# One transformer layer on one core: h, o and the merged tile in four tiles per half, o loaded block pair by block pair, and three merge weights split on VectorE

## The chip, the cores and the metric

The kernel runs on one core of a Trainium2 chip. A core has TensorE (matrix products into PSUM), VectorE, ScalarE and GpSimd (elementwise work), SyncE, whose queue issues most transfers, and 16 DMA engines shared by the transfer queues of SyncE, ScalarE and GpSimd. Each engine works through its own instructions in order and waits on semaphores for the others.

The metric is the device time of one execution in microseconds, the median of three. The profile is of one more execution. In its rows PE is TensorE, PEld its weight loads, DVE VectorE, ACT ScalarE, POOL GpSimd and SPq the transfers issued by SyncE; L12 is line 12 of the kernel.

## The reference

One layer works on 512 latent tokens (a grid of 8 x 64) and on 128 context tokens. Both groups go through the same weights. Cut to what matters here:

```python
h = _rmsnorm(x, p["norm1_g"]) * (1.0 + sc1) + sh1
u_rw, u_na, gate_rw, gate_na = jnp.split(h @ p["w_in"], IN_SPLITS, axis=-1)
o_rw, s_new = _rwkv_branch(u_rw, s0, ...)     # bidirectional recurrence, 8 heads of 64
q, k, v = jnp.split(u_na, 3, axis=-1)
...
o_na = _na_latent(q, k, v, ctx_k, ctx_v, p["na_rpb"])   # neighbourhood attention
merged = (jax.nn.sigmoid(gate_rw) * (o_rw @ p["w_o_rwkv"])
          + jax.nn.sigmoid(gate_na) * (o_na @ p["w_o_na"]))
x = x + g1 * (merged @ p["w_out"])
h2 = _rmsnorm(x, p["norm2_g"]) * (1.0 + sc2) + sh2
x = x + g2 * ((jax.nn.silu(h2 @ p["ffn_w1"]) * (h2 @ p["ffn_w3"])) @ p["ffn_w2"])
```

D_MODEL is 1024, so h, the merged tile and o (o_na and o_rw side by side, 512 features each) have 1024 features for 640 tokens.

## The kernel before

**High and low halves.** Every large product is made of three: an operand x is kept as hi, its rounding to TensorE's fast float format, and lo = x - hi, and w.x is hi.hi + hi.lo + lo.hi. So every activation tile comes twice. Features lie on the partitions: 1024 features are 8 blocks of 128, and a block has 640 columns, one for each token.

**h, o and m share their room.** The pool `hp` holds, one after the other, h (hi in `hh`, lo in `hl`), o (`o[0]`, `o[1]`) and the merged tile (`mh`, `ml`). Each of these is a `Two`: two tiles of four blocks (`hp_t`, line 334, `Two`, line 337, `hilo`, line 345). A tile of o takes the buffer of the tile of h with the same tag, and so can be loaded only when the last reader of that tile of h is done. o itself has waited in DRAM (`o_d`), since h is still needed while it is made; block 7 stays on the chip (`o3`).

**The stage around the change.** The recurrence goes through four channel groups ct, each in turn `main` (products for the chunk matrices), `inv` (inverting 32 x 32 blocks row by row on VectorE, 30 steps), `carry` (the sequential part) and `out` (normalisation, gate). TensorE's idle time between these is filled by a stream of independent products, `stream(order)`: projections (k, r, v, l), gates g0 to g15, then the merge products a0 to a3 (o_na by w_o_na, blocks 0 to 3 of o) and b0 to b3 (blocks 4 to 6). The table `plan` says how many products of the stream each step takes (`weave`), `tick` and `later` put the elementwise work of a product a few products behind it. The orders of TensorE, VectorE, ScalarE and GpSimd are those in which the program is written; a scheduler sets SyncE's.

**The last gate.** g14 is the last reader of h. Alone among the gates it goes through the blocks by pairs (`gate2_gen`, line 570): for each pair of blocks kts both halves of the tokens, six products each. After the pairs (0, 1) and (2, 3) it calls `o_load(0, 4)`, which issues eight transfers (hi and lo of blocks 0 to 3, 320 KB each). Blocks 4 and 5 are loaded when a0 is written (line 812), block 6 when the recurrence has stored it.

**Weights.** `wdma` (line 157) loads 512 KB into one of two buffers `wst`; `wcast` (line 178) makes hi by a ScalarE cast (line 185) and lo in one of two ways. With "p" in the table `wl`, ScalarE writes -w (line 183) and a GpSimd transfer of 512 KB adds w to it (line 184, `wlo<-wst` in the profile). With "d", VectorE subtracts (line 188). The buffer `wst` is free when cast and low half are done, and so the load of the weight after next waits for them. `wl` has one letter for each of the 39 units of the stream; letters 32 to 35 are those of a0 to a3.

In ct = 3 the lines to follow are: L579 the products of g14, L216 those of a and b, L1484 the loads of o, L164 the loads of merge weights, L1262 the transpose with which `inv` starts, L1293 and L1297 its steps, L1306 and L1308 the transposes at its end, L1137 and L1139 the bonus term, L1122, L1444, L1445, L1446 and L1448 the normalisation of the channel group before, L1216, L1239, L1188 and L1191 products for the chunk matrices (L1222 copies out the first of them), L1453 the gate product, L1319 and L1333 the products that join the inverted blocks, L1327 and L1338 the copies of the result.

Of the kernel before, what the change touches and what calls it, by code (L numbers as in the profile page):

```python
# [8 lines left out]
F32R = mybir.dt.float32r  # L9
# [5 lines left out]
P = 128  # L15
NT = 640
# [54 lines left out]
    h2=0.91, jobs=((2, 9, 28), (2, 9, 28), (2, 9, 28), (2, 8, 28)),  # L71
    mds=((4, 12), (4, 12), (4, 12), (4, 12)), bud=((1.8, 0.8), (1.3, 1.8)), off=6, tk=2, h3=1,
    h4=1.07, g1=2, km="dddddddd", kb="ddpd", ma="d", yo="pppd", r0="pd", rl=(0, 0, 0), lh=(0, 0, 1, 1),
    wl="dddddddddppppppppppppppppppppppppppdddd", nu=9, lg=14, jo=(2, 0, 1), na=(
        "6.0.12.0.1 6.0.12.0.0 6.0.12.0.0 6.0.12.0.2 6.0.12.0.0 6.0.12.0.2 6.0.12.0.0 6.0.12.0.2 6.0.12.0.0 "
        "6.0.12.0.2 6.0.12.1.0 6.1.12.1.2 6.2.12.2.0 6.1.12.2.2 6.0.12.2.0 6.1.12.1.2 6.2.14.2.0 "
        "6.2.14.1.2 6.2.14.2.0 6.2.14.2.0 6.3.18.2.0 10.0.10.0.0"))
# [30 lines left out]
def body(ctx: ExitStack, tc: tile.TileContext, xs, xp, cols, consts, w_ada, b_row, w_rw, w_qkv,  # L108
# [10 lines left out]
    def right_pool(stack, name):  # L119
        return stack.enter_context(tc.tile_pool(name=name, bufs=1, reuse_waits="tile", side="right"))  # L120
# [4 lines left out]
    hp = right_pool(hstack, "hp")  # L125
# [9 lines left out]
    def nm(s):  # L135
        cn[0] += 1
        return f"{s}_{cn[0]}"
# [34 lines left out]
    def later(fn, cost=(0.5, 0), more=0):  # L172
        if off[0]:
            pend.append([off[0] + more, cost, fn])
        else:
            fn()
# [155 lines left out]
    o, mt = [], []  # L332

    def hp_t(n, i, j):
        return hp.tile([P, 4, NT], F32R, tag=f"hp{i}{j}", bufs=1, name=f"{n}{i}{j}")

    class Two:

# [1 line left out]
            self.ts = ts  # L340

        def __getitem__(self, x):
            return self.ts[x[1] // 4][x[0], x[1] % 4, x[2]]

    def hilo(n):
        return [Two([hp_t(n, i, j) for j in range(2)]) for i in range(2)]

    hh, hl = hilo("h")

    s0 = ExitStack()  # L350
# [219 lines left out]
    def gate2_gen(i, w, ps_, gsb, gtag):  # L570
        dst = trw_d[i] if i < 8 else tna_d[i - 8]
        ps = [ps_(), None]
        for kts in ((0, 1), (2, 3), (4, 5), (6, 7)):
            for hf, (a, b) in enumerate(halves):
                if ps[hf] is None:
                    ps[hf] = ps_()
                for kt in kts:
                    for n, (u, x) in enumerate(((w[0], hh), (w[0], hl), (w[1], hh))):
                        pe.matmul(ps[hf][:, :H2], u[:, kt * 128:kt * 128 + 128], x[:, kt, a:b],  # L579
                                  start=kt == 0 and n == 0, stop=kt == 7 and n == 2)  # L580
                        yield
            if kts[1] == 3:
                o_load(0, 4)

        def rest(hf, a, b):
            t = gsb.tile([P, H2 if gtag == "fl" else 643], F32, tag=gtag, bufs=2, name=nm(gtag))[:, :H2]
            act.activation(t, ps[hf][:, :H2], AF.Tanh, scale=0.5)
            sp.dma_start(dst[:, a:b], t)

        for hf, (a, b) in enumerate(halves):  # L590
            later(lambda hf=hf, a=a, b=b: rest(hf, a, b))
# [192 lines left out]
    def stream(order):  # L784
# [10 lines left out]
        for i, g in enumerate(order):  # L795
            while wait.get(g) not in marks:
                yield False
            n, f = us[i][0], us[i][3]
            cast(i)
            it = f(ws[i])  # L800
            for j in range(n):
                if j == n // 8:
                    later(lambda i=i: cast(i + 1), (1.05, 0), -off[0])
                if j == (n // 2 if n == 48 else n // 4) and i + 2 < len(us):
                    ds.append(us[i + 2][1]())
                next(it)
                tick(1)
                if j == n - 1:
                    drain(it)
                    done.add(g)  # L810
                    if g == "a0":
                        o_load(4, 6)
                        if "O2" in marks:
                            o_load(6, 7)
                yield True
# [7 lines left out]
    with s1:  # L823
# [93 lines left out]
        with ExitStack() as s1b:  # L917
# [127 lines left out]
            with tc.manual_schedule(engines=FIRST):  # L1045
                for k, step in enumerate(PRM["na"].split()):
                    a, p, b, q, n = (int(x) for x in step.split("."))
# [29 lines left out]
    with ExitStack() as s3:  # L1077
# [397 lines left out]
        def o_load(a, b):  # L1475

            if not o:
                o.extend(Two([]) for _ in range(2))
            for q in sorted(set(range(a, b)) - got):
                got.add(q)  # L1480
                for i, (t, t_d) in enumerate(zip(o, o_d)):
                    if len(t.ts) == q // 4:
                        t.ts.append(hp_t("o", i, q // 4))
                    sp.dma_start(t[:, q, :].bitcast(F32), t_d[q])  # L1484

        def mt_tile(c8):
# [152 lines left out]
    pp = open_pool(ctx, "pp4", bufs=3, space=PSUM)  # L1639

    mh, ml = hilo("m")
    def last_gen():
        ts_ = []
# [44 lines left out]
    def add_gated(ps, i, n, c, a=0, b=512):  # L1688
# [15 lines left out]
                      name=f"b{x[0]}{x[1]}{i}") for i in range(2)] for x in halves2}  # L1704
# [390 lines left out]
```

## Time and profile before

| | us |
|---|---|
| median of 3 runs | 1171.59 (1171.57 to 1172.24) |
| the profiled execution, its own time | 1170.39 |
| its span, first to last instruction | 1168.6 |
| TensorE busy in the span | 1123.1 |
| VectorE busy | 775.6 |
| ScalarE busy | 535.4 |
| GpSimd busy | 194.3 |
| mean granted TensorE clock | 0.992 |

The profiled execution's own time is 1.2 us below the median of the three runs. A row of a timeline gives the start, the time, the engine, the line, the operation, what it writes and reads, and in brackets how long the engine had been idle before and what ended that; products are pipelined, so their times overlap. A row of a table by stretches gives for each engine the busy time and the number of instructions, then the clock granted to TensorE, the busy share of the DMA engines and the rate.

### The profile page before, as it was taken

To read this page: it belongs to the slowest core of one execution; us is meant where nothing else is said; L and a number is where in the kernel's file an instruction comes from. 1 tells how busy PE (TensorE), PEld (TensorE's weight loads), DVE (VectorE), ACT (ScalarE), POOL (GpSimd) and SP (SyncE) were. 2 spreads that over 40 slices of the span, in tenths; PEclk is the share of its full clock that TensorE was granted. 3 is DMA by queue.
4 is the path that set the end of the run, shared out by engine and by line. 5 is a ranking of instruction groups with operands and counts; after the bars stand their busy time and mean duration, and the time that the engine had idled before them with its cause. 6 is when DMAs were issued, how large, how long until landed. Compare 5 with 4: busy or idle time off the path is not lost.

```text
span 1168.6 us, 26884 instructions
## 1 busy us (share of the span) xinstructions
PE 1123.1 (96%) x11160; PEld 995.0 (85%) x11160; DVE 775.6 (66%) x1639; ACT 535.4 (46%) x1054; POOL 194.3 (17%) x264
## 2 busy tenths in 40 slices
PE   6999999999999999999899899989999999999998
PEld 4688877789888988888788778989899989998997
DVE  4565365569558847945577856877567756875775
ACT  4444566554565665557353424644224423441330
POOL 1163244320101212110200241100000000001000
PEclk9999999999999999999999999999999999999999
DMA  9752777654433433343843772322212321232122
GB/s 338 259 117 81 229 245 226 200 145 117 110 85 88 133 82 91 105 107 91 276 130 108 239 217 67 96 73 85 97 54 91 100 87 67 73 108 90 54 83 98
DMA packets 60770, 150.21 MB, mean 129 GB/s; under 512 B 7492, under 2 KB 22468, under 8 KB 60648
## 3 DMA queue, kind: packets, MB, share of 16 engines
q1 hardware_dynamic: 55464, 131.56, 34.4%
q0 software_dynamic: 4320, 15.73, 6.9%
q8 instruction: 88, 1.44, 0.5%
q10 hardware_dynamic: 864, 1.20, 0.4%
q14 instruction: 34, 0.28, 0.1%
HBM read 118.41 MB, written 14.32 MB: 114 GB/s over the span
## 4 chain that ended last, share of the span: by engine, by line
PE 60%; DVE 7%; issue 7%; ACT 3%; DMA 1%; SPq 0%; POOL 0%; DVEq 0%; ACTq 0%; POOLq 0%
PE f L1814 23%; PE acc L303 16%; PE fl L216 10%; DVE pr L1293 1%; PE mm L216 1%; PE w L1394 1%; DVE RL L1297 1%; PE w L1367 1%; PE w L1191 1%; PE w L1407 1%; DMA o<-o_d 1%; PE w L1379 1%; PE w L1169 1%; ACT wlo L183 1%; PE w L1239 0%
## 5 line engine op out<-in xcount | busy, mean ns | idle before, releaser
L1814 PE MATMUL f<-t,whi 128*128 128x320 f32 x640 | 141.4, 309 | 0.0
L1814 PE MATMUL f<-b,whi 128*128 128x320 f32 x608 | 136.4, 312 | 3.6 <-ACT b L204 1.8
L303 PE MATMUL acc<-whi,u 128*128 128x512 f32 (+1 forms) x448 | 135.9, 385 | 0.0
L216 PE MATMUL fl<-h,whi 128*128 128x320 f32 x672 | 121.3, 320 | 0.8 <-issue 0.8
L1814 PEld LDWEIGHTS f<-t,whi 128*128 128x128 f32 x640 | 106.9, 188 | 0.0
L1814 PEld LDWEIGHTS f<-b,whi 128*128 128x128 f32 x608 | 102.7, 189 | 4.7 <-ACT b L204 2.2
L216 PEld LDWEIGHTS fl<-h,whi 128*128 128x128 f32 x672 | 101.5, 188 | 5.5 <-issue 0.9
L185 ACT CAST whi<-wst 128x1024 fp32r<-128x1024 f32 (+1 forms) x77 | 79.1, 1033 | 56.1 <-PE acc L303 42.5
L1814 PE MATMUL f<-t,wlo 128*128 128x320 f32 x320 | 98.9, 309 | 0.0
L303 PEld LDWEIGHTS acc<-whi,u 128*128 128x128 f32 x448 | 83.5, 188 | 16.6
L1814 PE MATMUL f<-b,wlo 128*128 128x320 f32 x304 | 94.6, 311 | 1.4 <-DVE wlo L1858 1.4
L1855 ACT CAST whi<-ws 128x1024 fp32r<-128x1024 f32 x40 | 42.0, 1050 | 108.4 <-PE f L1814 48.2
L303 PE MATMUL acc<-wlo,u 128*128 128x512 f32 (+1 forms) x224 | 86.3, 385 | 0.0
L1869 POOL TENSOR_TENSOR ws<-wst 128x512 f32<-128x512 f32 x20 | 28.0, 1402 | 341.3 <-DVE wlo L1858 247.7
L188 DVE TENSOR_TENSOR wlo<-wst,whi 128x1024 fp32r<-128x1024 f32 (+2 forms) x55 | 58.3, 1072 | 31.8 <-ACT whi L185 31.2
L303 PE MATMUL acc<-whi,h 128*128 128x512 f32 x240 | 78.5, 401 | 0.8 <-DVE h L428 0.8
L1691 DVE SCALAR_TENSOR_TENSOR tt<-acc,G 128x512 f32<-128x512 f32 (+1 forms) x51 | 34.7, 680 | 59.3 <-PE acc L303 45.3
L216 PE MATMUL fl<-h,wlo 128*128 128x320 f32 x336 | 63.5, 321 | 0.0
L1855 ACT CAST whi<-wst 128x1024 fp32r<-128x1024 f32 (+1 forms) x48 | 41.3, 868 | 42.3 <-PE acc L303 25.1
L1814 PEld LDWEIGHTS f<-t,wlo 128*128 128x128 f32 x320 | 60.1, 188 | 0.0
L1858 DVE TENSOR_TENSOR wlo<-ws,whi 128x1024 fp32r<-128x1024 f32 x40 | 55.0, 1374 | 6.3 <-ACT whi L1855 6.3
L1814 PEld LDWEIGHTS f<-b,wlo 128*128 128x128 f32 x304 | 57.6, 190 | 1.7 <-DVE wlo L1858 1.7
(342 smaller groups left out, 2512.8 us busy)
## 6 DMA issues: line engine op xcount, KB each, us to landing
wst<-in_w_dram SPq DMA_DIRECT2D x66, 512.0 KB
wst<-in_w_rw_dram SPq DMA_DIRECT2D x31, 512.0 KB
wlo<-wst POOLq DMA_DIRECT2D x30, 512.0 KB, 4.6
wa<-in_w_ada_dram SPq DMA_DIRECT2D x24, 512.0 KB
f<-in_w_ada_dram SPq DMA_DIRECT2D x16, 512.0 KB
wst<-in_w_qkv_dram SPq DMA_DIRECT2D x12, 512.0 KB
o<-o_d SPq DMA_DIRECT2D x14, 320.0 KB
x<-in_xs_dram SPq DMA_DIRECT2D x8, 512.0 KB
```

What stands on the lines that cost most here:

```text
L183: act.activation(lo[:, :n], st[:, :n], AF.Copy, scale=-1.0)
L185: act.copy(hi[:, :n], st[:, :n])
L188: dve.tensor_tensor(out=lo[:, a:b], in0=st[:, a:b], in1=hi[:, a:b].bitcast(F32), op=ALU.subtract)
L216: pe.matmul(ps[:, :t1 - t0], w[:, a:a + 128], x[:, k0 + kt, t0:t1], start=n == 0, stop=n == 3 * nk - 1)
L303: pe.matmul(pss[i][:, a:b], lhs(x, kt, ts_), w[:, cs_], start=ki == 0 and n == 0, stop=ki == last and n == 2)
L1169: pe.matmul(t[r0:r0 + 32, 64 * i:64 * i + 64], S.BK[l // 10][own, l % 10, 0, 32 * bk:32 * bk + 32], V(AG[own, l, h, :], [[0, 2], [1, 32]], ...
L1191: pe.matmul(pr[h][hrows[h ^ i], o_], x[hrows[h], :], R_[hrows[h], l, :], start=True, stop=True)
L1691: dve.scalar_tensor_tensor(out=tt, in0=ps[:, a:b], scalar=c, in1=G[:, g, sl], op0=ALU.mult, op1=ALU.mult)
L1814: pe.matmul(ps[:, :H2], w_[:, c_], x_[:, kt, :], start=first and kt + n == 0, stop=last and kt == 3 and n == 2, skip_group_check=more)
L1855: act.copy(r[0][:, :width], src())
L1858: dve.tensor_tensor(out=r[1][:, :width], in0=src(), in1=r[0][:, :width].bitcast(F32), op=ALU.subtract)
L1869: eng_x(PRM["se"][i - 1]).tensor_tensor(out=o_, in0=x, in1=y, op=op)
```

## The change

Three edits. The tiles of the pool `hp` have two blocks instead of four, so h, o and m are four tiles each for hi and lo, in the same room. The loads of o are issued in pairs: after g14 has used blocks 0 and 1 the four transfers of these blocks, after blocks 2 and 3 theirs; the loads of blocks 4 and 5 keep their place in the program but now need only the third tile of h. And in `wl` the letters of a0, a1 and a2 become "d": their low halves are made by VectorE, without the ScalarE copy and the GpSimd transfer.

```diff
@@ PRM
-    wl="dddddddddppppppppppppppppppppppppppdddd", ...
+    wl="dddddddddppppppppppppppppppppppdddpdddd", ...
@@ hp_t, Two, hilo
-        return hp.tile([P, 4, NT], F32R, tag=f"hp{i}{j}", bufs=1, name=f"{n}{i}{j}")
+        return hp.tile([P, 2, NT], F32R, tag=f"hp{i}{j}", bufs=1, name=f"{n}{i}{j}")
...
-            return self.ts[x[1] // 4][x[0], x[1] % 4, x[2]]
+            return self.ts[x[1] // 2][x[0], x[1] % 2, x[2]]
...
-        return [Two([hp_t(n, i, j) for j in range(2)]) for i in range(2)]
+        return [Two([hp_t(n, i, j) for j in range(4)]) for i in range(2)]
@@ gate2_gen
-            if kts[1] == 3:
-                o_load(0, 4)
+            if kts[1] < 4:
+                o_load(kts[0], kts[0] + 2)
@@ o_load
-                    if len(t.ts) == q // 4:
-                        t.ts.append(hp_t("o", i, q // 4))
+                    while len(t.ts) <= q // 2:
+                        t.ts.append(hp_t("o", i, len(t.ts)))
```

TensorE's order is the same product by product. Two queues change. First SyncE's, at the loads of o, with what each transfer waits for (PE, DVE, Activation: the counters of those engines; DMAHW and DMASW with a number: an earlier transfer of SyncE's and of GpSimd's queue). Before:

```order
L1484 DMA o_7606<-o_d_81 128x640 [waits PE_49]
L1484 DMA o_7604<-o_d_80 128x640 [waits DMAHW7_49,PE_49]
L1484 DMA o_7604<-o_d_80 128x640 [waits DMAHW0_49]
L1484 DMA o_7606<-o_d_81 128x640 [waits DMAHW1_49]
L1484 DMA o_7604<-o_d_80 128x640 [waits DMAHW2_49]
L1484 DMA o_7606<-o_d_81 128x640 [waits DMAHW3_49]
L1484 DMA o_7604<-o_d_80 128x640 [waits DMAHW4_49]
L1484 DMA o_7606<-o_d_81 128x640 [waits DMAHW5_49]
L164 DMA wst_7926<-in_w_o_dram 128x2x512 [waits DMAHW6_49,DMASW6_49,Activation_49]
L588 DMA tna_d<-fl_7731 128x320 [waits DMAHW7_49,Activation_49]
```

And with the change:

```order
L1484 DMA o_7587<-o_d_81 128x640 [waits PE_49]
L1484 DMA o_7585<-o_d_80 128x640 [waits DMAHW7_49,PE_49]
L1484 DMA o_7585<-o_d_80 128x640 [waits DMAHW0_49]
L1484 DMA o_7587<-o_d_81 128x640 [waits DMAHW1_49]
L164 DMA wst_7930<-in_w_o_dram 128x2x512 [waits DMAHW2_49,DVE_49]
L1484 DMA o_7615<-o_d_81 128x640 [waits DMAHW3_49,PE_49]
L1484 DMA o_7613<-o_d_80 128x640 [waits DMAHW4_49,PE_49]
L1484 DMA o_7613<-o_d_80 128x640 [waits DMAHW5_49]
L1484 DMA o_7615<-o_d_81 128x640 [waits DMAHW6_49]
L1484 DMA o_7946<-o_d_81 128x640 [waits DMAHW7_49,PE_49]
L1484 DMA o_7943<-o_d_80 128x640 [waits DMAHW0_49,PE_49]
```

The load of a2's weight (`wst<-in_w_o_dram`) now stands between the two groups of four and waits for VectorE (a0's low half) where it waited for ScalarE and GpSimd's transfer; blocks 4 and 5 follow at once, ahead of g14's stores (`tna_d<-fl`).

Second VectorE's order, in `inv` of ct = 3 at the fifth and sixth steps. Before:

```order
L1293 TENSOR_TENSOR pr_7596<-RL_7560 128x65 x2
L1297 TENSOR_TENSOR RL_7560<-RL_7560,pr_7596 128x13x5 x2
L1139 TENSOR_TENSOR bv_7329<-w_7716,vp_623 128x320
L1293 TENSOR_TENSOR pr_7596<-RL_7560 128x72
L1293 TENSOR_TENSOR pr_7596<-RL_7560 128x78
```

And with the change:

```order
L1293 TENSOR_TENSOR pr_7605<-RL_7564 128x65 x2
L1297 TENSOR_TENSOR RL_7564<-RL_7564,pr_7605 128x13x5 x2
L188 TENSOR_TENSOR wlo_7744<-wst_7611,whi_7743 128x1024
L1139 TENSOR_TENSOR bv_7333<-w_7721,vp_627 128x320
L1293 TENSOR_TENSOR pr_7605<-RL_7564 128x72
```

The low half of a1 has come in ahead of the bonus term. Those of a0 and a2 stand, in the same way, right behind the transpose of L1262 and at step 17 of the inversion (128x119), each as one row more.

More of the change, by code (lines that the diff above doesn't have):

```diff
@@ L73 @@
     h4=1.07, g1=2, km="dddddddd", kb="ddpd", ma="d", yo="pppd", r0="pd", rl=(0, 0, 0), lh=(0, 0, 1, 1),
-    wl="dddddddddppppppppppppppppppppppppppdddd", nu=9, lg=14, jo=(2, 0, 1), na=(
+    wl="dddddddddppppppppppppppppppppppdddpdddd", nu=9, lg=14, jo=(2, 0, 1), na=(
         "6.0.12.0.1 6.0.12.0.0 6.0.12.0.0 6.0.12.0.2 6.0.12.0.0 6.0.12.0.2 6.0.12.0.0 6.0.12.0.2 6.0.12.0.0 "
```

## The prediction

> **What bounds the kernel now.** I read the page first, then the chain of waits around the loads of o, then the timelines of TensorE, SyncE, VectorE and ScalarE there, and last the tables by stretches.
>
> ```profile
> span 1168.6 us, 26884 instructions
> PE 1123.1 (96%) x11160; PEld 995.0 (85%) x11160; DVE 775.6 (66%) x1639; ACT 535.4 (46%) x1054; POOL 194.3 (17%) x264
> ```
>
> TensorE is busy for 96% of the span, so time can be won only where it stands still or runs slowly, and each such place counts once. The chain of waits from 545 to 605 us shows one:
>
> ```profile
> 561.08 1.24 SPq L1484
> 562.37 6.88 DMA o<-o_d
> 569.29 1.55 PE fl L216 x5
> 570.85 1.07 PE w L1122 x5
> ...
> 579.46 11.59 PE fl L216 x78
> ```
>
> For 6.88 us the kernel hangs on the transfers of o. TensorE's timeline there:
>
> ```profile
> 554.41 0.31 PE L579 MATMUL fl<-h,wlo 128*128 128x320 f32 x1
> ...
> 557.29 0.31 PE L579 MATMUL fl<-h,wlo 128*128 128x320 f32 x1
> ...
> 563.08 0.55 PE L579 MATMUL fl<-h,wlo 128*128 128x320 f32 x1
> 563.79 0.53 PE L216 MATMUL fl<-o,whi 128*128 128x320 f32 x2 [0.15 <-DMA o<-o_d]
> ...
> 569.29 0.49 PE L216 MATMUL fl<-o,whi 128*128 128x320 f32 x1 [0.85 <-DMA o<-o_d]
> ...
> 575.34 0.38 PE L1191 MATMUL w<-R__2897,f 64*64 64x64 f32 x9 [0.23 <-ACT ZV L1222]
> ```
>
> At full pace a product takes 11.59/78 = 0.15 us. The last product of h starts at 563.08, so the eighth product of o could start at 563.23 + 7 x 0.15 = 564.3. It starts at 569.29: 5.0 us late. The loads were issued when blocks 0 to 3 of h were done (557.29 + 0.31 = 557.6):
>
> ```profile
> 553.56 0.32 SPq L566 DMA_DIRECT2D tna_d<-fl  x1
> 557.49 5.32 SPq L1484 DMA_DIRECT2D o<-o_d  x8
> 562.91 0.64 SPq L164 DMA_DIRECT2D wst<-in_w_o_dram  x1
> ```
>
> The tables by stretches show why they took so long (the DMA share and the rate are the last two columns; the two queue rows are of 557.4 to 560 and of 560 to 569.3, with packets, MB and share):
>
> ```profile
> 553.56:554.36 0.80, 0.77 (x5) 0.78 (x6) 0.80 (x1) 0.80 (x1) 0.00 (x0) 1.00 0.00 0
> 554.36:555.20 0.84, 0.84 (x8) 0.84 (x7) 0.47 (x2) 0.84 (x2) 0.54 (x4) 1.00 0.52 195
> ```
> ```profile
> q0 software_dynamic: 112, 0.46, 104.7%
> ```
> ```profile
> q1 hardware_dynamic: 1459, 3.18, 97.4%
> ```
>
> A store issued at 553.56 begins to move 0.8 us later. The loads issued from 557.49 on moved nothing until 560: GpSimd's queue, which is a0's accumulating transfer, held the 16 engines. Then SyncE's queue moved 3.18 MB in 9.3 us, 0.342 MB/us, so a load of o (0.328 MB) takes 0.96 us and a weight (0.524 MB) 1.53 us. Eight loads from 560 would be through at 567.7; the eighth product started 1.6 us after that, which I keep as the tail of a landing.
>
> The wait has a second price, read from the granted clock (the column before the DMA share):
>
> ```profile
> 562.66:566.08 3.42, 2.31 (x9) 1.18 (x8) 1.08 (x5) 2.34 (x4) 0.68 (x1) 1.00 0.95 319
> 566.08:569.49 3.41, 1.46 (x5) 0.75 (x5) 0.00 (x0) 0.00 (x0) 0.24 (x1) 1.00 1.00 355
> 569.49:572.90 3.41, 3.41 (x12) 2.51 (x11) 1.16 (x5) 0.24 (x1) 0.00 (x0) 0.50 1.08 281
> ```
>
> After a stretch with TensorE busy for 1.46 of 3.41 us the clock is 0.50 for the next 3.41 us; after 2.31 busy it stayed 1.00.
>
> **The change part by part. Tiles of two blocks and loads by pairs.** The first four loads need only blocks 0 and 1 of h, done at 554.41 + 0.31 = 554.7 instead of 557.6. They move from 554.7 + 0.8 = 555.5, on engines that are then free: the accumulating transfer of a0 is gone with the third edit. But SyncE's queue now has a2's weight ahead of the second four, 1.53 us more. So the ninth piece is through at 555.5 + 8 x 0.96 + 1.53 = 564.7, and with the tail of 1.6 the eighth product starts at 566.3, 3.0 us earlier than now. Without a tail it would be 564.7. That SyncE is blocked is not a risk on this reckoning: a2's weight waits for a0's low half on VectorE (555.8, below), and the loads behind it wait for TensorE until 557.6 anyway. The loads of blocks 4 and 5 and the stores of g14 come behind and are used much later.
>
> The stage of h and that of the merged tile have the finer tiles too. TensorE's waits there stay as they are in the order; I cost them at nothing, and the most they could give or take is a wait like this one:
>
> ```profile
> L303 PE MATMUL acc<-whi,h 128*128 128x512 f32 x240 | 78.5, 401 | 0.8 <-DVE h L428 0.8
> ```
>
> **Low halves on VectorE.** Removed are three ScalarE copies of 1.05 us and three GpSimd transfers; added are three subtractions on VectorE, 1.22 us each by their median:
>
> ```profile
> L188 DVE TENSOR_TENSOR wlo<-wst,whi x55: 674/1218/1251, 18.5 to 1142.2; 128x1024 fp32r<-128x1024 f32 x35, 128x512 fp32r<-128x512 f32 x16, 128x768 fp32r<-128x768 f32 x4
> ```
> ```profile
> 553.30 1.25 DVE L1262 STREAM_TRANSPOSE RL<-Nt 128x1024 f32<-128x1024 f32 x1 [2.75 <-ACT Nt L1174]
> ...
> 556.95 0.17 DVE L1112 TENSOR_SCALAR r<-w 128x10 f32<-128x10 f32 x1 [2.08 <-PE w L1108]
> ...
> 563.53 0.49 DVE L1139 TENSOR_TENSOR bv<-w,vp 128x320 f32<-128x320 f32 x1 [1.56 <-PE w L1137]
> ...
> 564.22 0.38 DVE L1297 TENSOR_TENSOR RL<-RL,pr 128x72 f32<-128x72 f32 x2
> 571.74 0.69 DVE L1444 TENSOR_TENSOR out<-out,w 128x512 f32<-128x512 f32 x1 [7.14 <-PE w L1122]
> ```
> ```profile
> 553.43 1.05 ACT L183 ACTIVATE wlo<-wst 128x1024 fp32r<-128x1024 f32 x1
> ...
> 564.06 1.05 ACT L183 ACTIVATE wlo<-wst 128x1024 fp32r<-128x1024 f32 x1
> 565.00 1.03 ACT L185 CAST whi<-wst 128x1024 fp32r<-128x1024 f32 x1
> ...
> 574.11 1.18 ACT L1222 COPY ZV<-w 64x512 f32<-64x512 f32 x2 [0.53 <-PE w L1216]
> ```
>
> a0's low half follows the transpose, 554.55 to 555.8, in the 2.08 us that VectorE idles before 556.95: nothing (1.22 if TensorE released L1112 at once). a1's must wait for its cast, which moves up to where the copy stood, 564.06 + 1.03 = 565.1; the low half ends at 566.3. Queued behind it are L1139 and step 6 of the inversion, 563.53 to 564.6 now, hence 566.3 to 567.4, and behind these L1444, which TensorE, ScalarE and the next chunk products wait for. Now L1444 waits until 571.74, so most of this is hidden; it would cost up to 2.8 us if TensorE came at once.
>
> When would TensorE let L1444 go? Now it is 571.74 - 569.29 = 2.45 us after the eighth product, at half clock. At full clock the four low products and five transposes take about half, so I take 1.4 us (bounds 1.2 and 2.45): 566.3 + 1.4 = 567.7, just behind VectorE's 567.4. From there to the product at 575.34, which waits for ScalarE's copy L1222, pass 575.34 - 571.74 = 3.6 us, of them 0.53 in which ScalarE waited for the slow TensorE. So that product starts at 567.7 + 3.6 - 0.53 = 570.8: **4.5 us** gained (3.0 transfers, 1.0 and 0.5 clock).
>
> a2's low half falls between steps 16 and 17 of the inversion, when VectorE is full. What hides it:
>
> ```profile
> 603.15 0.96 DVE L188 TENSOR_TENSOR wlo<-wst,whi 128x768 fp32r<-128x768 f32 x1 [0.76 <-ACT whi L185]
> ...
> 608.63 0.89 DVE L1338 COPY Rt<-w 32x320 f32<-32x320 f32 x2 [0.95 <-ACT Rt L1338]
> ```
>
> VectorE idles 0.76 + 0.95 = 1.7 us at the end of the inversion, more than 1.22. Without that cover it would cost the 1.22. In exchange TensorE no longer waits for a2's transfer:
>
> ```profile
> 592.48 0.86 PE L216 MATMUL fl<-o,wlo 128*128 128x320 f32 x4 [0.27 <-DMA wlo<-wst]
> ```
>
> That is 0.3 us more. Sum: 4.5 + 0.3 = **4.8 us**. Behind 610 us TensorE is the bound and everything moves up with it. The profiled execution took 1170.39 in all (span 1168.6 and 1.8 around it), so it would take 1165.6; it lies 1.2 below the median of the runs, so the forecast for the median is 1171.59 - 4.8 = **1166.8**. Between a tail of nothing (VectorE's 567.4 then decides, 0.3 more) and one that is 1.5 longer, its own range is 1165.5 to 1168.5.
>
> The Trainium skill (TensorE: Matmul & The Clock Gate, Part 1) states that the clock gate watches a free-running window of about 3.4 us and halves the clock after one idle window. The rows of 566.08 and 569.49 agree in length and factor, and the page adds what one trace cannot show: the window's place changes from run to run. By the three stretches alone the sum is 4.8; by the page it is 4.8 or, where the window falls badly, 3.3.
>
> **Rivals.** (1) The transfers stay late. The weight ahead of the second four costs 1.53 us by itself; if the tail doubles too (+1.6), the eighth product starts at about 568, the slow clock stays, and the gain is 1.3 + 0.3 = 1.6 to 2.5: about 1169.5. For it: the queue is 97.4% full. Against: its engines are free at 555.5. (2) The clock drops all the same. TensorE still stands from 563.2 to 566.3 with a few products; if a stretch of 3.41 us lies just there, the 1.5 us of clock are not won: 1168.3. Against it is the first of the three stretches, 2.31 busy at 1.00. This is the page's rule with the window shifted. (3) More: no tail, so that VectorE's 567.4 decides (5.1 us), and one slow stretch further on falls away because everything behind has moved, half of 3.41 us:
>
> ```profile
> 729.90:733.33 3.43, 1.66 (x7) 0.95 (x6) 1.89 (x8) 2.65 (x9) 0.00 (x0) 1.00 0.82 257
> 733.33:736.74 3.41, 3.15 (x12) 3.05 (x12) 3.34 (x8) 1.29 (x3) 0.00 (x0) 0.50 0.12 26
> ```
>
> That makes 6.8: 1164.8. Against it: a stretch can as well appear as go. (4) The edits don't do what they say: the pairs come free no earlier in effect, since everything waits for the queue, and only the 0.3 us remains: 1171.3. (5) Slower: VectorE becomes the bound of the inversion. If the loads land no earlier and the three low halves, at the 1.37 us that L1858's like subtraction takes, stand uncovered in its chain, they cost 4.1 - 1.7 = 2.4 us: 1174. It decides from the point where the copies behind 603.15 end later than the 0.95 us of idle at 608.63 allow.
>
> ```profile
> L1858 DVE TENSOR_TENSOR wlo<-ws,whi 128x1024 fp32r<-128x1024 f32 x40 | 55.0, 1374 | 6.3 <-ACT whi L1855 6.3
> ```
>
> Against it: the first two low halves fall in idle of 2.08 and 7.14 us.
>
> **How the numbers follow.** Forecast 0.55, (1) 0.15, (2) 0.12, (3) 0.08, (4) 0.05, (5) 0.05. The range of 1164.6 to 1169.7 holds the forecast, (2), (3) and most of (1). A measurement of this kernel tells about 0.2% (2.3 us) from no change, so faster means below 1169.25: the forecast, (2), (3) and half of (1), 0.83; the same: the other half of (1) and (4), 0.12; slower: (5), 0.05.
>
> **What would show it.** In the changed profile the first four loads of o are issued near 554.7, the eighth product of o starts near 566.3, and no clock of 0.50 follows. L1444 starts at 567.4 to 568 with a1's low half just ahead of it, the product of L1191 near 570.8, and there is no wait for `wlo` at the start of a2. Wrong would be: an eighth product after 568, L1444 waiting long for VectorE's own queue, or idle of TensorE at 600 to 610 that ends on VectorE's copies.

## The result, and the profile after

The changed kernel took 1166.0 us (median of 7 runs, 1163.2 to 1169.57), the kernel before 1171.57 in the same comparison. The ratio of the runs is 0.9958, 95% interval 0.9947 to 0.9970: a gain of 4.9 us, between 3.5 and 6.2 (the medians lie 5.6 apart). The profiled execution took 1167.39, 3.0 less than that of before. Its page begins:

```profile
span 1165.6 us, 26873 instructions
PE 1119.1 (96%) x11160; PEld 992.5 (85%) x11160; DVE 778.7 (67%) x1642; ACT 532.4 (46%) x1051; POOL 191.2 (16%) x261
```

The 3.0 us of the two profiled executions understate the gain, because the transpose L1262 with which `inv` of ct = 3 starts came 1.58 us later in the changed kernel's execution (554.88 against 553.30). No effect of the finer tiles shows in this: over all profiles below the transpose lies between 551.7 and 555.7 with them and between 551.7 and 555.4 without them. What makes it scatter is not shown. From here on all times are therefore counted from that transpose: **"+13.3" is 13.3 us behind its start**. TensorE's order is the same in both kernels, so its rows can be compared one by one. The timeline of TensorE after (start, time, what, and in brackets the idle time ahead and its cause):

```profile
564.66 0.56 PE L579 MATMUL fl<-h,wlo 128*128 128x320 f32 x1
565.05 0.75 PE L216 MATMUL fl<-o,whi 128*128 128x320 f32 x4
566.68 0.56 PE L216 MATMUL fl<-o,whi 128*128 128x320 f32 x2 [0.87 <-DMA o<-o_d]
567.49 0.41 PE L216 MATMUL fl<-o,whi 128*128 128x320 f32 x1 [0.25 <-DMA o<-o_d]
568.22 0.41 PE L216 MATMUL fl<-o,whi 128*128 128x320 f32 x1 [0.32 <-DMA o<-o_d]
...
572.78 0.38 PE L1191 MATMUL w<-R__2901,f 64*64 64x64 f32 x9 [0.35 <-ACT ZV L1222]
...
589.49 0.75 PE L216 MATMUL fl<-o,wlo 128*128 128x320 f32 x4
```

The first four products of o now start at once behind the last of h, where each used to wait; 1.44 us of waiting for loads are left. The eighth stands at +13.34 (before 569.29 - 553.30 = +15.99), the waiting product of L1191 at +17.90 (before +22.04), and a2's first low product, now without a wait, at +34.61 (before 592.48 - 553.30 = +39.18). So 4.57 us are gained up to a2. Behind it both profiles take 572.0 us to TensorE's last product: the gain is kept, and 4.57 - 1.58 is the 3.0 of the two executions. A second profile of the kernel before (e11) has a2 at +38.97. Two more profiles of the changed kernel (e10, and e12, which differs from it only behind a2) have it at +34.98 and +34.21. So the gain up to a2 is 4.0 to 5.0 us.

SyncE's timeline and the tables by stretches (busy time of the engines, then clock, DMA share, rate) show the loads:

```profile
556.19 1.74 SPq L1484 DMA_DIRECT2D o<-o_d  x4
558.03 0.38 SPq L164 DMA_DIRECT2D wst<-in_w_o_dram  x1
559.07 6.26 SPq L1484 DMA_DIRECT2D o<-o_d  x8
```
```profile
555.17:559.50 4.33, 4.33 (x32) 4.33 (x32) 3.29 (x6) 0.88 (x1) 1.47 (x7) 1.00 0.61 201
559.50:561.50 2.00, 2.00 (x99) 1.74 (x98) 1.52 (x10) 1.19 (x5) 1.83 (x1) 1.00 0.77 225
561.50:565.05 3.55, 3.55 (x24) 3.39 (x23) 2.03 (x8) 1.48 (x4) 0.00 (x0) 1.00 1.00 378
565.05:568.47 3.42, 1.98 (x10) 1.23 (x9) 1.76 (x4) 1.37 (x2) 0.00 (x0) 1.00 1.03 409
568.47:572.78 4.31, 3.96 (x115) 3.38 (x114) 3.17 (x13) 2.13 (x4) 0.00 (x0) 1.00 1.05 396
```

The first load is issued at +1.31 and its data begin to move at +2.26; what moves ahead of them is a store issued at 555.14, so the 0.61 of the first stretch is in part time in which no load could move yet. From 559.5 to 561.5 the engines are not full, from 561.5 on they are. The clock stays at 1.00 through the wait and behind it. VectorE's timeline in the same place:

```profile
566.71 1.23 DVE L188 TENSOR_TENSOR wlo<-wst,whi 128x1024 fp32r<-128x1024 f32 x1 [3.17 <-ACT whi L185]
567.85 0.48 DVE L1139 TENSOR_TENSOR bv<-w,vp 128x320 f32<-128x320 f32 x1
...
569.69 0.69 DVE L1444 TENSOR_TENSOR out<-out,w 128x512 f32<-128x512 f32 x1 [0.78 <-PE w L1122]
```

a1's low half and what is queued behind it are through 0.78 us before TensorE releases L1444: it is covered, barely.

### The profile page after: what moved, and what is told of

The parts are those of the page before. It is cut to its first block, busy times and chain, and to the rows that moved or that the text cites. A ratio compares the mean times of both kernels' runs of the same rounds, so it can differ in the third digit from the quotient of the medians.

```text
span 1165.6 us, 26873 instructions
## 1 busy us (share of the span) xinstructions
PE 1119.1 (96%) x11160; PEld 992.5 (85%) x11160; DVE 778.7 (67%) x1642; ACT 532.4 (46%) x1051; POOL 191.2 (16%) x261
## 3 DMA queue, kind: packets, MB, share of 16 engines
q8 instruction: 88, 1.44, 0.5%
## 4 chain that ended last, share of the span: by engine, by line
PE 60%; DVE 8%; issue 6%; ACT 3%; DMA 1%; POOL 0%; SPq 0%; DVEq 0%; ACTq 0%; POOLq 0%
PE f L1814 22%; PE acc L303 17%; PE fl L216 10%; PE mm L216 1%; DVE pr L1293 1%; PE w L1394 1%; DVE RL L1297 1%; PE w L1367 1%; PE w L1191 1%; DMA o<-o_d 1%; PE w L1407 1%; PE w L1379 1%; PE w L1169 1%; ACT wlo L183 1%; DVE hq L1773 1%
## 5 line engine op out<-in xcount | busy, mean ns | idle before, releaser
L188 DVE TENSOR_TENSOR wlo<-wst,whi 128x1024 fp32r<-128x1024 f32 (+2 forms) x58 | 62.0, 1080 | 35.0 <-ACT whi L185 34.5
```

Source lines behind the costliest of these rows:

```text
L188: dve.tensor_tensor(out=lo[:, a:b], in0=st[:, a:b], in1=hi[:, a:b].bitcast(F32), op=ALU.subtract)
```

## The experiments

Lines in kernels with added code are shifted by a few (L1451 there is L1444, L1198 is L1191, L1664 is L1655). All ratios are against runs of the kernel before on the same chip. The times forecast for e1, e2, e3, e5, e6, e9 and e12 were all missed, the measured ones being 0.2 to 3.6 us longer: what follows rests on the rows of the profiles, and few of the times tell these kernels apart.

**e1 and e7: tiles and pairs without the letters.**

```diff
-    wl="dddddddddppppppppppppppppppppppdddpdddd"
+    wl="dddddddddppppppppppppppppppppppppppdddd"
```

> Tiles of two blocks and loads by pairs, the letters of a0 to a2 as before (ScalarE copy and GpSimd transfer). All times are counted from the start of the transpose L1262 of ct = 3; in the kernel before the eighth product of o comes 15.99 us after it and the product of L1191 that waits for L1222 22.04, in the changed kernel 13.34 and 17.90. My theory, two halves of one gain: the loads start early, but a0's accumulating transfer still holds the engines for some 2.5 to 2.9 us, so the eighth product comes at 14.3 to 15.0, the half clock may stay, TensorE's 0.3 us wait for a2's low half is back, time 1168.5 to 1170. Rival 'the tiles carry all': 13.3 and 17.9, time 1166.3. Rival 'the letters carry all': 16.0 and 22.0, time 1171.5.

> e1_tiles once more, for a second profile. In the first, TensorE lost 2.2 us between 668 and 680 us to VectorE's L1655 (1.80 us for one that otherwise takes 1.17), far behind the change, which made the kernel slower than the kernel before although it had gained 1.0 us at a2. If that belongs to the edit, the product that stands 1.57 us later than the forecast of the rows before comes late again by 2 us (from the product of index 8200 to that of 8400 in TensorE's order 44.6 us instead of 42.5); if it is an accident of a run, 42.5. At a2's first product the same as in e1, 38.2 after the transpose.

Measured: ratio 1.0012 (0.9999 to 1.0024), a median of 1172.44, so no gain. The eighth product came at +14.57 and +14.18, near the 14.3 to 15.0 of my theory, and a2's first low product at +38.18 and +38.42: only 0.8 to 1.0 us gained of 4.57. In e1 the clock fell once more (stretches chosen to match its windows), and a2 waited for its transfer in both:

```profile
567.60:571.00 3.40, 1.66 (x7) 1.17 (x8) 0.00 (x0) 0.88 (x1) 0.92 (x1) 0.99 1.03 328
571.00:574.40 3.40, 3.40 (x26) 2.49 (x26) 1.66 (x7) 0.92 (x1) 0.00 (x0) 0.50 0.97 231
```
```profile
593.92 0.85 PE L216 MATMUL fl<-o,wlo 128*128 128x320 f32 x4 [0.36 <-DMA wlo<-wst]
```

In e7 the clock stayed up, but TensorE stopped for a reason that comes up again below:

```profile
574.80 0.37 PE L1191 MATMUL w<-R__2901,f 64*64 64x64 f32 x9 [1.55 <-issue]
...
592.01 0.85 PE L216 MATMUL fl<-o,wlo 128*128 128x320 f32 x4 [1.02 <-DMA wlo<-wst]
```

The loss of 2.2 us at the merge stands in e1 and not in e7, so it does not come with every execution of this kernel. Whether it is why twelve runs gain nothing stays open.

**e2 and e8: the letters alone.** The first two edits undone:

```diff
-        return hp.tile([P, 2, NT], F32R, tag=f"hp{i}{j}", ...)
+        return hp.tile([P, 4, NT], F32R, tag=f"hp{i}{j}", ...)
...
-            if kts[1] < 4:
-                o_load(kts[0], kts[0] + 2)
+            if kts[1] == 3:
+                o_load(0, 4)
```

> Only the letters: low halves of a0, a1, a2 on VectorE; tiles of four blocks and all eight loads after block 3 as before. Counted from the transpose L1262 of ct = 3. SyncE has a2's weight ahead of all eight loads here, and that weight moves before they are issued. My theory: engines free at the issue, so the eighth product comes at 14.0 to 14.6 (half of the gain), L1191's product at 18.6 to 20, time 1167.5 to 1169. Rival 'the tiles carry all': 16.0 and 22.0, and only the 0.3 us of a2 gained, time 1171.3. Rival 'the letters carry all': 13.3 and 17.9, time 1166.3.

> e2_letters once more, for a second profile. Same question as in e7: 44.6 us again from the 8200th to the 8400th product if the loss of 2.2 us at the merge belongs to the edit, 42.5 if it is an accident of a run. At a2's first product 37.0 to 38.5 after the transpose, as the clock falls (it stood at half for 6.8 us in the first profile, at 568.7).

Measured: ratio 0.9992 (0.9979 to 1.0006), a median of 1169.94, so no gain clear of noise. Eighth product at +14.95 and +14.70, a little later than forecast; L1191's product at +21.72 and +19.27; a2's first low product at +38.43 and +36.70, 0.8 and 2.5 us gained. In e2 the clock was 0.50 for two stretches behind the loads, in e8 it was not. The half-clock stretches of an execution all start on one grid of 3.413 us (last section). Cut along the grid, the stretch ahead of the fall in e2 has TensorE busy for 2.14 us, and the two over the same work in e8 for 2.59 and 2.24:

```profile
565.30:568.70 3.40, 2.14 (x9) 1.11 (x7) 1.43 (x2) 1.37 (x2) 0.00 (x0) 0.99 1.00 367
568.70:572.10 3.40, 2.81 (x8) 2.07 (x9) 0.78 (x5) 0.00 (x0) 0.00 (x0) 0.50 1.04 406
572.10:575.50 3.40, 3.40 (x33) 2.54 (x34) 2.15 (x7) 0.92 (x1) 0.00 (x0) 0.50 1.04 406
```
```profile
560.91:564.33 3.42, 2.59 (x12) 1.58 (x10) 0.78 (x1) 1.57 (x3) 0.00 (x0) 1.00 0.99 349
564.33:567.74 3.41, 2.24 (x13) 1.68 (x13) 1.43 (x6) 0.00 (x0) 0.00 (x0) 1.00 1.04 401
```

Neither rival holds: each half brings the eighth product 1.0 to 1.8 us forward, both together 2.65, and only both together bring the whole 4.57.

**e3: a0's letter alone, with the tiles.**

```diff
-    wl="dddddddddppppppppppppppppppppppdddpdddd"
+    wl="dddddddddppppppppppppppppppppppdpppdddd"
```

> The changed kernel with the letters of a1 and a2 back to ScalarE copy and GpSimd transfer; a0 stays on VectorE. Counted from the transpose L1262 of ct = 3. My theory: a0's letter alone frees the engines for the loads of o, so the eighth product stays at 13.3; L1444 comes up to 0.5 us earlier since VectorE has no low half of a1 ahead of it; a2's wait of 0.3 us comes back; time 1165.8 to 1166.8, the same as the changed kernel. Rival 'VectorE's low half of a1 bounds': L1191's product 0.5 to 1.2 us earlier than 17.90, time 1165. Rival 'a1's accumulating transfer collides with the loads behind the eighth': L1191's product within 0.3 of 17.9, but later waits of TensorE for loads or for a1's low half of over 1 us, time 1167.5 or more.

Measured: ratio 0.9987 (0.9976 to 0.9997), a median of 1168.96. The eighth product (565.11 - 551.73 = +13.38) and L1191's (+17.95) are those of the changed kernel: a0's letter alone frees the loads. But a2 stands at +36.63, 2.0 us later, in two places:

```profile
571.26 0.37 PE L1191 MATMUL w<-R__2901,f 64*64 64x64 f32 x9 [0.66 <-issue]
588.36 0.85 PE L216 MATMUL fl<-o,wlo 128*128 128x320 f32 x4 [0.92 <-DMA wlo<-wst]
```

The third rival comes nearest, with L1191 in place, more than 1 us lost behind it and a time above 1167.5, but the waits are others than it named. From the stop without a releaser on, TensorE is 0.93 us later than in the changed kernel, and the wait for a2's low half (not for a1's or for loads) adds 1.09; that wait was 0.27 in the first profile of before and none in e11. So the letters of a1 and a2 bring nothing at the loads, but are worth two microseconds behind them. The runs agree: the intervals of e3 and of the changed kernel, each against before, do not overlap.

**e4: a2's weight behind the loads.**

```diff
+                    hold_sp[0] = g == "a0"
                     ds.append(us[i + 2][1]())
+                    hold_sp[0] = False
...
+        if hold_sp[0]:
+            tc.keep_in_program_order(sp.dma_start(...))
```

> The changed kernel with a2's weight load kept behind the loads of blocks 0 to 5 in SyncE's queue (nothing else moves). Counted from the transpose L1262 of ct = 3. My theory: the queue ahead of the second four loads is one weight shorter, so the eighth product comes 1.2 to 1.5 us earlier, at 11.9 to 12.1; but then VectorE's low half of a1, the bonus term and step 6 let L1444 start only 0.8 us earlier, so L1191's product is at 17.1 and the time 0.8 us below that of the changed kernel (1165.2). Rival 'the weight moves in a gap of the queue': the eighth product at 13.0 to 13.3, time as the changed kernel. Rival 'VectorE does not bind': L1191's product at 16.5, time 1164.6.

Measured: ratio 0.9963 (0.9949 to 0.9977). Eighth product at 564.39 - 552.12 = +12.27, 1.07 earlier than in the changed kernel's first profile; L1444 at 566.09, +13.97, with no idle ahead of it; L1191's product at +17.05. All that lies within 0.2 us of the forecast, and yet a2 stands at +34.77, no earlier than in the changed kernel, and the ratio is no better either. TensorE stopped in the middle of the small products with nothing to wait for:

```profile
566.41 0.97 PE L1223 MATMUL w<-K,vp 64*64 64x64 f32 x26
...
570.88 0.36 PE L1198 MATMUL w<-R__2901,f 64*64 64x64 f32 x9 [0.79 <-issue]
```

The tables of the DMA queues (packets, MB, share of the engines) for 566.4 to 568.4 and for 568.4 to 569.4 show what it lacked. One packet of 16 KB of instructions (q8) comes only then, behind a data queue that takes all of the engines:

```profile
q1 hardware_dynamic: 476, 0.76, 105.0%
```
```profile
q1 hardware_dynamic: 194, 0.38, 100.0%
q8 instruction: 1, 0.02, 5.8%
```

**e5: blocks 4 and 5 out of the way as well.** On top of e4:

```diff
-                    if g == "a0":
+                    if g == "a1":
                         o_load(4, 6)
```

Two more edits keep these loads in that place of SyncE's queue and block 6 behind them.

> The kernel e4_weight_behind with the loads of blocks 4 and 5 moved from the end of a0 to the end of a1, so that in SyncE's queue they stand behind a3's weight. Counted from the transpose L1262. In e4 TensorE stood in the middle of the L1188/L1191 products with nothing to wait for in the profile, until 18.76 (18.60 in the changed kernel, where these products started 0.8 us later), and the 16 KB packet of instructions that it would need next began to move only at 16.34, 2.05 us after TensorE had passed the start of that group, while the data queue was full. My theory: the instruction packet is late because the engines are full of loads; with blocks 4 and 5 out of the way it begins by 15.5, the stop ends by 17.9 and the first product of a2 comes at 33.7 to 33.9 instead of 34.77; time 0.9 us below e4. Rival 'the stop is TensorE's own and has nothing to do with the queue': it ends at 18.6 to 18.8 again, a2 at 34.8, time as e4. Rival 'blocks 4 and 5 come late for b0': a wait for loads of over 0.3 us at b0, time above e4.

Measured: ratio 0.9957 (0.9944 to 0.9969). The stop is gone, and a2 is at 587.32 - 553.57 = +33.75, the forecast. The same tables, for 565.8 to 567.8 and 567.8 to 568.8: the data queue has room, and the packet comes at 567.85, ahead of the products of 567.99 (in e4 2.05 us behind them).

```profile
q1 hardware_dynamic: 284, 0.53, 84.1%
```
```profile
q1 hardware_dynamic: 71, 0.14, 71.2%
q8 instruction: 1, 0.02, 5.8%
```

The stop is gone in e6 and e9 too, which contain this edit. The time, forecast 0.9 us below that of e4, was 1166.47 against 1165.47, with nearly the same ratio. In the profile the merge took 44.7 us from TensorE's 8200th to its 8400th product instead of 42.5.

**e6: all moves.** On top of e5 the loads of blocks 2 and 3 by token halves, and a1's cast eight products later:

```diff
+            for (u, v) in halves:
+                for q in sorted({2, 3} & set(range(a, b))):
+                    for t, t_d in zip(o, o_d):
+                        sp.dma_start(t[:, q, u:v].bitcast(F32), t_d[q][:, u:v])
...
-                if j == n // 8:
+                if j == (14 if g == "a0" else n // 8):
```

> e5_blocks_late, and in addition the loads of blocks 2 and 3 are split by token halves (the first half of all four tiles first), and a1's cast and low half are asked for eight products later. Counted from the transpose L1262. My theory: the eighth product needs half of the last four loads and comes at 11.3 to 11.7 instead of 12.3; L1444 no longer stands behind a1's low half and follows at 12.8 to 13.2 (13.97 in e4), the waiting product of L1191 at 16.0 to 16.4 (17.05 in e4); what is left of it at a2 depends on the instruction packet, which must begin by 14.4: a2's first product between 32.9 and 33.8; time 1163.6 to 1164.6. Rival 'the instructions bound': a2 no earlier than in e5, time as e5. Rival 'small transfers': 160 KB loads move so much slower that the eighth product is no earlier than 12.2.

Measured: ratio 0.9968 (0.9953 to 0.9984), a median of 1168.21. TensorE no longer waits for loads at all: eighth product at +11.20, L1191's at +15.67, earlier than forecast. But a2 is at +34.00, later than in e5. A new wait, which I had not seen:

```profile
578.85 1.44 PE L221 MATMUL fl<-o,whi 128*128 128x320 f32 x8 [1.51 <-ACT mt L1539]
```

ScalarE's copy `mt` that empties a PSUM buffer stands behind the cast of L209, which waits 2.42 us for VectorE, where a1's low half now comes first.

**e9 and e12: the merge.** The profiles of e1, e2, e5, e6, e8 and e10 lose 2.2 us or more there, those of before, e11, after, e3, e4 and e7 do not. In e9 (on top of e5) and e12 (the changed kernel) the subtractions of the merged tile leave GpSimd:

```diff
-                pool.tensor_tensor(out=ml[:, c8, a:b], ...)
+                dve.tensor_tensor(out=ml[:, c8, a:b], ...)
```

> e5_blocks_late with the low halves of the merged tile (the subtraction behind the cast in the last merge stage, 16 of them) on VectorE instead of GpSimd. In e5, e6, e2, e8 and e1 TensorE lost 2.2 us there (44.7 us from its 8200th to its 8400th product instead of 42.5), with VectorE's sums of mt and the gate taking 0.48 to 1.85 us each while GpSimd worked. My theory: VectorE's sum waits for GpSimd's subtraction when both run; without it all sums take 0.48 us, and although VectorE gets 16 x 0.48 more the stretch takes at most 42.5 us, so that e5's microsecond at a2 (33.75) comes through to the end: time 1163.5 to 1164.8. Rival 'VectorE becomes the bound': the 7.7 us more on VectorE make the stretch 43 us or longer; time 1166 or more. Rival 'the loss has another cause': sums still at 1.2 us and more, the stretch 44.7.

> The changed kernel with nothing but the 16 low halves of the merged tile moved from GpSimd to VectorE (no move of loads). The changed kernel had 42.5 us from TensorE's 8200th to its 8400th product in one profile and 45.1 in the other (with the clock at half for 3.4 us in that stretch). If the merge loss comes from VectorE and GpSimd working at once, the stretch is 41.9 as in e9, the sums of L1655 all take 0.48 us, a2's first low product stays at 34.6 to 35.0 after the transpose L1262, and the time is 0.9 us above e9's and 0.6 to 2.5 below the changed kernel's: 1163.5 to 1165.9. If e9's gain came from the later loads and not from this, 42.5 or 44.7 and 1166.

The durations (minimum, median, maximum in ns) of VectorE's sum there, in e5 and in e9:

```profile
L1664 DVE TENSOR_TENSOR tr<-P,tr x4: 476/1232/1853, 667.0 to 672.4; 128x320 f32<-128x320 f32 x4
L1664 DVE TENSOR_TENSOR tr<-kk,tr x2: 1169/1187/1205, 673.0 to 674.9; 128x320 f32<-128x320 f32 x2
```
```profile
L1664 DVE TENSOR_TENSOR tr<-P,tr x4: 484/484/487, 668.2 to 672.2; 128x320 f32<-128x320 f32 x4
L1664 DVE TENSOR_TENSOR tr<-kk,tr x2: 484/484/484, 673.0 to 674.6; 128x320 f32<-128x320 f32 x2
```

The stretch takes 41.9 us in both e9 and e12. Where GpSimd keeps the subtractions, the eight sums of this stretch show one of two patterns, which go with 44.7 us (two sums of 1.8 us at the start, as in e5) and with 42.5 us (one of 3.1 us, as in before and after): the longest single sum belongs to the shorter stretch. e9 runs in 1164.98 us, ratio 0.9941 (0.9924 to 0.9959), the lowest of the study; its interval overlaps that of the changed kernel. e12 has 0.9969 (0.9955 to 0.9983), no better than the changed kernel, although its one profile (a2 at +34.21, span 1163.0) is 2.6 us shorter, 1.6 of them ahead of the transpose. Its 12 runs lie between 1163.28 and 1171.62, and their median of 1167.65 is above the forecast range. So what the merge costs in a profile is shown; what it is worth in the median is not.

**e10 and e11: the changed kernel and the kernel before once more.**

> The changed kernel once more, for a second profile. The gain up to a2 belongs to the edits: its first product 34.5 to 34.8 after the transpose L1262 again. From the 8200th to the 8400th product 42.5 us if the loss at the merge never strikes this kernel, 44.7 if it does; half-clock stretches elsewhere at other places than in the first profile (246.1, 345.1, 730.8 us).

> The kernel before once more, for a second profile. a2's first product at 38 to 39.5 after the transpose L1262 (39.18 in the first, with the clock at half for 3.4 us behind the loads of o); if the half clock there depends on where its windows fall, it can be 1.5 us less. From the 8200th to the 8400th product 42.5 or 44.7 us.

a2's first low product came at +34.98 (after) and +38.97 (before): 4.0 us between them, 4.57 in the first pair. The eighth product came at +13.36 and +16.00. The two executions took 1170.33 and 1171.29; the former is above all seven runs of the first comparison. The changed kernel's second profile has the merge loss (45.1 us, with the clock at half for 3.4 us of it), so the edit does not protect it from that.

## Why the prediction was right

The median of 1166.0 lies 0.8 us below the forecast of 1166.8, and the steps came out one by one, counted from the transpose (first profile):

| step | forecast | measured |
|---|---|---|
| first load of o issued | +1.4 | +1.31 |
| eighth product of o | +13.0 | +13.34 |
| half clock behind it | none | none |
| L1444 | +14.4 | +14.81 |
| waiting product of L1191 | +17.5 | +17.90 |
| a2's first low product | +34.4 | +34.61 |

The steps bear the prediction out. That the median came so near is in part luck: the seven runs lie between 1163.2 and 1169.57, and the times forecast for the experiments did far worse than their rows. One bound was wrong as well. With a tail of nothing the prediction's own terms give 1171.59 - 4.8 - 0.3 = 1166.5, where it says 1165.5. The median lies 0.5 below that; by the ratio of the runs the gain is 4.9, so this is scatter of the medians as far as can be told.

**Transfers:** 3.0 forecast, 15.99 - 13.34 = 2.65 measured. The start was right (data move from +2.26, forecast +2.2) and so was the end; in between, two errors offset each other, which is luck. I let the first four loads pass at 0.96 us each, which with the tail puts the fourth at +7.6. It had landed only at 563.27 (+8.39). In return a2's weight ahead of the second four cost less than my 1.53: moving it away in e4 gave 1.07, and three profiles without it there (e4, e5, e9) have the eighth product 0.9 us earlier in the mean than three with it (after, e10, e12). What slowed the first loads is open, but it is no property of the order. In e12, with the same loads issued at the same times, the engines stay full where the changed kernel's first profile has 0.77, the fourth load is there at +7.63 and the eighth product at +12.63:

```profile
557.91:559.91 2.00, 2.00 (x99) 1.74 (x98) 1.52 (x10) 1.19 (x5) 1.83 (x1) 1.00 1.01 352
```
```profile
565.92 0.41 PE L216 MATMUL fl<-o,whi 128*128 128x320 f32 x1 [0.36 <-DMA o<-o_d]
```

The tail of 1.6 has a measured counterpart. The sixteen parts of the eighth load, one for each DMA engine, landed between 566.54 and 568.18: TensorE waits for the slowest engine.

**Clock:** 1.0 + 0.5 forecast, (22.04 - 17.90) - 2.65 = 1.49 measured. None of the three profiles (after, e10, e12) has half clock behind the loads. That it can go either way, as rival (2) has it, is shown for the letters alone by e2 and e8, the same kernel with 6.8 us of half clock there and with none. Here the page "TensorE: Matmul & The Clock Gate" (Part 1) of the Trainium skill agrees with the runs in this: the window's place changes between executions, so the busy time of a stretch that is cut elsewhere does not decide. In another it does not: the prediction quotes it for one idle window ahead of the halving, and the window ahead of the fall in e2 held 2.14 us of work (more of this in the last section).

**VectorE:** a1's low half was priced at nothing because it would end just before TensorE's release, and it ended 0.78 us before. e4 shows the price beyond that point: there L1444 starts without idle, and of 1.07 us gained at the eighth product 0.85 arrive at L1191. a0's and a2's cost nothing visible.

**a2's transfer:** 0.3 forecast, 4.57 - 4.14 = 0.43 measured, but e11, the same kernel before, has no wait there at all. This is the one term whose meaning I had wrong. I took it as a small wait that goes. Without the letters of a1 and a2 it would have cost 1.1 us, and TensorE would have stopped besides and lost 0.9 (e3). The sum did not need it, since the edit removes the one, and the other cost at most 0.4 us in the changed kernel's profiles (e10).

**The rivals.** The weight ahead of the second four (1) delayed less than priced, and the tail did not double. (3), a larger gain, did not come in the profile: there is a tail, and a half-clock stretch still stands at 730.8. (4), that the pairs do nothing since everything waits for the queue, is refuted by e1 (eighth product 1.4 and 1.8 us earlier without the letters). Whether the call by pairs matters beside the finer tiles is not shown: all runs with the tiles have both. (5), VectorE as the bound, did not come: the changed kernel's TensorE shows no wait between a2's first low product and 610 us.

## What to carry to other kernels

A resource that stands in one place several times over (here the DMA engines: an accumulating transfer, loads released late, a weight) has to be cleared of all of them: the tiles alone gained 0.8 to 1.0 us up to a2, the letters alone 0.8 to 2.5, and neither any time clear of noise in the runs; both together gained 4.0 to 5.0. Count from a common instruction that the edit does not touch, not from the span's start, and compare row by row; that resolves about 0.8 us, the spread of these rows over three profiles of the changed kernel, where runs scatter by several. And when a wait goes, look for the next late thing on the same DMA engines: here it was TensorE's own instructions.

## What the hardware showed that I had not expected

**Instructions compete with data for the DMA engines.** Packets of 16 KB of instructions (q8) pass through the same engines, 88 of them in the changed kernel's profile, for some 22500 instructions of TensorE: 256 for each packet. In e3, e4, e7 and e8 TensorE, which here passes a 64 x 64 product every 0.03 us or so, stopped for 0.50 to 1.55 us and went on 2.2 to 2.4 us after the packet had begun to move (568.85 to 571.26, 568.46 to 570.88, 572.44 to 574.80, 570.20 to 572.40). It stopped ahead of the same product each time, number 7068 in TensorE's order, and so it did in e1, e10 and e12, for 0.10 to 0.13 us. The profile says only "issue", and that the packet holds that product's instruction is inferred. In e5, e6 and e9, with fewer loads queued, the packet was early and the stop gone, so the cause is shown by removing it.

**VectorE and GpSimd hold each other up.** A sum of two SBUF operands on VectorE took 0.48 us with GpSimd's subtractions moved away and up to 3.1 us (first profile of the changed kernel) beside them; in e9 and e12 it took 0.48 every time. The Trainium skill ("SBUF — State Buffer", section "SBUF: two separate sides") says that the two share a port pair that one of them holds for a whole instruction while the other blocks; e9 and e12 agree, though they do not show the lock itself. What the runs add is that the pattern falls into one of two states with the same instructions, 42.5 or 44.7 us for the stretch; what decides between them stays open.

**The windows of the clock lie on a grid, and a window need not be idle.** In each of the 14 profiles all half-clock stretches start a whole number of 3.413 us apart. In before they start at 23.36, 234.99, 344.21, 569.49, 733.33 and 1166.82: 62, 32, 66, 48 and 127 such steps. The grid lies elsewhere in the next execution (569.49 in before, 567.51 in e11). Cut along it, from 30 us on, the windows at full clock in which the profile has TensorE busy for less than 1.5 us were all followed by half clock (17 windows, 1.21 to 1.48 us), and none with more than 2.2 us was. In between both happened: 2.16 us led to half clock in e2, and 1.51 us did not in e6.
